# A two-layer encoder in fp32 halves on one core: modulation in 1 MB units, norm chains without other work in them, the MLP in three parts

## The chip, the core and the metric

The kernel runs on one core of a Trainium2 chip. The metric is the device time of one execution in microseconds, read as the median of several runs. The engines are called by their names in the profile: PE (TensorE, matmuls), PEld (its weight loads), DVE (VectorE), ACT (ScalarE), POOL (GpSimd) and SP (SyncE, whose one queue issues every transfer here).

## The reference

One sequence of 256 tokens with 2048 features passes through two layers. Cut to what matters:

```python
c_act = jax.nn.silu(c)
for layer in range(2):
    mod = c_act @ ada_w[layer] + ada_b[layer]            # 2048 x 12288
    sh1, sc1, g1, sh2, sc2, g2 = jnp.split(mod, 6, axis=-1)
    h = rmsnorm(x, norm_mix[layer]) * (1.0 + sc1) + sh1
    proj = h @ w_in[layer]                               # 2048 x 4608
    ...  # 8 heads of differential attention, 8 of windowed attention
    x = x + g1 * (jnp.concatenate([out_a, out_b], -1) @ w_out[layer])
    h2 = rmsnorm(x, norm_mlp[layer]) * (1.0 + sc2) + sh2
    x = x + g2 * (jnp.square(jax.nn.relu(h2 @ w_up[layer])) @ w_down[layer])
return rmsnorm(x, final_norm)                            # D_FF is 8192
```

All of it is float32. The weights and the modulation matrices are read once, 581.66 MB in all.

## The kernel before, in words

**Layout and arithmetic.** The activations lie transposed: features on the 128 partitions, the 256 tokens along a row. The residual stream is eight tiles of two 128-feature chunks each (`X`, in the trace `x`). A matmul in full precision is made of cheaper ones: each operand is cut into a high half, rounded to fp32r, and a low half that is the rest. For weights `split` makes them: ACT casts the high half (L367, `whi`), DVE subtracts it from the raw tile (L368, `wlo`). A weight tile is 0.5 MB, 128 x 1024. `gemm` (L383) loads one tile after another, splits it and gives each to PE; for the kind "s", which all the MLP uses, PE makes two products for each 128 columns: the high half times both halves of the activations (L408, 512 columns) and the low half times the high one (L410, 256 columns). It takes the chunks of the contraction in groups of four. `grouped_gemm` (L710) runs several column blocks over groups of chunks, and `settle` adds up what the groups gave.

**Modulation.** The product of the conditioning vector and the modulation matrix isn't made on PE: DVE multiplies a tile of the matrix by the activated vector, spread over the partitions, and sums each row in one operation (L255, `tensor_tensor_reduce`), which gives 128 values of the modulation. A unit of 128 outputs is 1 MB; `ada_job` (L237) loads it in two halves of 0.5 MB and sums them one after the other, the second starting from the first one's result. There are 384 halves. They are spread through the program by a planner: `feed` (L272) is called after every weight tile and issues the next half when enough credit has gathered; `pace` sets the credit per tile so that a goal (the table `GOALS`, in halves issued) is reached at the end of a stage; `cap` holds the planner back ahead of a group; `need` (L280) issues at once what a step must have.

**A layer.** `mixer` (L766) norms `x`, modulates it, projects it (in groups of 2, 4, 4 and 6 chunks in layer 0, all 16 in layer 1), makes the attention and projects back; `residual` (L752) adds the result to `x` with four DVE operations for each pair of chunks (L761). `mlp` (L838) does the hidden 8192 features in two parts of 4096 (`PARTS`): up projection, squared relu (`fin_up`: one DVE operation at L854, then a cast on ACT and a subtraction on DVE in `hilo`), down projection, `residual`.

**The norm chain.** In the last pass of a stage `residual` also squares each finished tile (`square_sum`, L526: ACT squares, DVE adds the first six up, L534, and PE makes the means, L541). `norm_x` (L545) then makes the reciprocal root: two ACT operations and four of DVE (L552 to L555). `modulated` (L573) applies it chunk by chunk: for the first tile in two halves, DVE multiplies (L585), ACT makes the high half (L589), ACT or DVE the exact value (L593, L591), DVE the low half (L595). PE waits for this ahead of every mixer and MLP.

**Buffers and order.** Weight tiles and modulation halves share the six buffers of `rawp`; the split halves have eight in `wp`, the activations 24 in `bp`. The order on each engine is made by a scheduler from the program's order and priorities (`tc.high_priority` for the norm chain); SP issues the loads in its order and stops where a load's buffer isn't free, with all later loads behind it. A sum, a split and a residual step that stand on DVE in one order run in that order.

## Time and profile before

| | |
|---|---|
| runs | 2314.43 us median of 3 (2310.29 to 2318.74) |
| profiled execution | 2310.85 us, of which the span of the trace is 2309.1 |
| mean granted clock of PE | 0.98 of 2.4 GHz |
| busy | PE 2191.3 us (95%), PEld 1894.8, DVE 1808.1 (78%), ACT 1061.2 (46%) |
| transfers | 585.96 MB, 254 GB/s over the span |
| chain that ended last | PE 83%, DVE 4%, ACT 2%, DMA 1% |

PE is busy nearly all the time; the rest of the span has to be looked for stage by stage. The rows below come from five views. The windows give for each stretch its length, then each engine's busy us with its number of instructions in brackets, then the granted clock of PE as a share of full speed, the share of the DMA engines' time that packets took, and GB/s. The groups give line, engine, operation, the output and input tiles and their shapes, the count, then busy us and the mean of one in ns, then the idle time ahead of them and what ended it. The timelines give the start in the span, the length, and in brackets the idle time of that engine just before and its releaser. The DMA issues give the tiles, the queue, how many, the size and the median time from issue to landing. In the first layer the mixer lies in about 0 to 450 us and the MLP behind it up to 1195; the second layer's mixer runs to 1567, its MLP to 2295.

### The profile page before, as it was taken

To read this page: it belongs to the slowest core of one execution; us is meant where nothing else is said; L and a number is where in the kernel's file an instruction comes from. 1 tells how busy PE (TensorE), PEld (TensorE's weight loads), DVE (VectorE), ACT (ScalarE), POOL (GpSimd) and SP (SyncE) were. 2 spreads that over 40 slices of the span, in tenths; PEclk is the share of its full clock that TensorE was granted. 3 is DMA by queue.
4 is the path that set the end of the run, shared out by engine and by line. 5 is a ranking of instruction groups with operands and counts; after the bars stand their busy time and mean duration, and the time that the engine had idled before them with its cause. 6 is when DMAs were issued, how large, how long until landed. Compare 5 with 4: busy or idle time off the path is not lost.

```text
span 2309.1 us, 33300 instructions
## 1 busy us (share of the span) xinstructions
PE 2191.3 (95%) x12540; PEld 1894.8 (82%) x12540; DVE 1808.1 (78%) x2698; ACT 1061.2 (46%) x1521; POOL 0.2 (0%) x4
## 2 busy tenths in 40 slices
...
GB/s 324 327 311 275 217 255 201 293 329 301 204 274 316 316 317 328 314 338 348 312 302 192 246 182 157 211 290 236 297 282 233 185 195 186 192 191 187 195 184 110
DMA packets 162450, 585.96 MB, mean 254 GB/s; under 512 B 18289, under 2 KB 18801, under 8 KB 162289
## 3 DMA queue, kind: packets, MB, share of 16 engines
...
HBM read 581.66 MB, written 2.10 MB: 253 GB/s over the span
## 4 chain that ended last, share of the span: by engine, by line
PE 83%; DVE 4%; ACT 2%; issue 1%; DMA 1%; ACTq 0%; DVEq 0%
PE acc L408 48%; PE acc L410 25%; PE acc L381 2%; PE acc L379 2%; PE acc L380 2%; PE misc L616 1%; DVE wlo L368 1%; PE lg L631 1%; DVE araw L255 1%; DVE x L761 1%; PE misc L608 1%; PE lg L680 1%; DMA raw<-in_w_up_dram 0%; ACT whi L367 0%; PE misc L562 0%
## 5 line engine op out<-in xcount | busy, mean ns | idle before, releaser
L408 PE MATMUL acc<-b,whi 128*128 128x512 f32 x4992 | 1742.5, 395 | 38.8 <-DVE b L595 29.4
L410 PE MATMUL acc<-b,wlo 128*128 128x256 f32 x4992 | 1377.1, 281 | 5.0 <-DVE wlo L368 4.8
L408 PEld LDWEIGHTS acc<-b,whi 128*128 128x128 f32 x4992 | 933.4, 188 | 249.2 <-issue 38.0
L367 ACT CAST whi<-raw 128x1024 fp32r<-128x1024 f32 x711 | 726.7, 1052 | 871.8 <-PE acc L408 540.0
L368 DVE TENSOR_TENSOR wlo<-raw,whi 128x1024 fp32r<-128x1024 f32 x711 | 851.9, 1222 | 321.5 <-ACT whi L367 319.4
L410 PEld LDWEIGHTS acc<-b,wlo 128*128 128x128 f32 x4992 | 943.5, 189 | 25.1 <-DVE wlo L368 11.9
L255 DVE CUSTOM_DVE_ANT_0 araw<-araw,c_act,vecs 128x1024 f32<-128x1024 f32 x192 | 249.1, 1303 | 43.5 <-DMA araw<-in_ada_dram 43.3
L255 DVE CUSTOM_DVE_ANT_0 araw<-araw,c_act,mod 128x1024 f32<-128x1024 f32 x192 | 249.1, 1303 | 35.5 <-DMA araw<-in_ada_dram 35.1
L761 DVE SCALAR_TENSOR_TENSOR x<-acc,mod,x 128x256 f32<-128x256 f32 x256 | 112.9, 480 | 24.1 <-PE acc L410 22.1
L379 PE MATMUL acc<-b,whi 128*128 128x256 f32 x320 | 92.1, 291 | 2.9 <-ACT whi L367 2.9
L380 PE MATMUL acc<-b,whi 128*128 128x256 f32 x320 | 91.8, 290 | 0.0
L381 PE MATMUL acc<-b,wlo 128*128 128x256 f32 x320 | 89.4, 293 | 2.5 <-DVE wlo L368 2.4
L487 ACT COPY tmp<-acc 128x256 f32<-128x256 f32 x120 | 44.5, 372 | 64.6 <-PE acc L410 64.3
L488 DVE TENSOR_TENSOR tmp<-tmp,acc 128x256 f32<-128x256 f32 x152 | 62.0, 418 | 14.0 <-ACT tmp L487 13.8
L498 ACT CAST b<-tmp 128x512 fp32r<-128x512 f32 x72 | 44.8, 623 | 49.8 <-DVE tmp L854 48.9
L379 PEld LDWEIGHTS acc<-b,whi 128*128 128x128 f32 x320 | 62.6, 196 | 4.9 <-ACT whi L367 3.3
L381 PEld LDWEIGHTS acc<-b,wlo 128*128 128x128 f32 x320 | 61.1, 197 | 5.3 <-DVE wlo L368 4.0
L380 PEld LDWEIGHTS acc<-b,whi 128*128 128x128 f32 x320 | 62.7, 196 | 1.1 <-issue 1.0
L380 PE MATMUL acc<-wlo,b 128*128 128x512 f32 (+1 forms) x152 | 56.6, 372 | 3.1 <-DVE wlo L368 3.0
L530 ACT ACTIVATE tmp<-x 128x512 f32<-128x512 f32 x35 | 21.7, 631 | 75.7 <-DVE x L761 68.3
L381 PE MATMUL acc<-whi,b 128*128 128x512 f32 (+1 forms) x152 | 55.9, 367 | 0.0
L499 DVE TENSOR_TENSOR b<-tmp,b 128x512 fp32r<-128x512 f32 x72 | 49.3, 688 | 7.1 <-ACT b L498 6.2
(156 smaller groups left out, 1258.6 us busy)
## 6 DMA issues: line engine op xcount, KB each, us to landing
araw<-in_ada_dram SPq DMA_DIRECT2D x384, 512.0 KB, 5.2
raw<-in_w_up_dram SPq DMA_DIRECT2D x256, 512.0 KB, 4.5
raw<-in_w_down_dram SPq DMA_DIRECT2D x256, 512.0 KB, 4.6
raw<-in_w_in_dram SPq DMA_DIRECT2D x144, 512.0 KB, 4.7
raw<-in_w_out_dram SPq DMA_DIRECT2D x64, 512.0 KB, 4.7
...
```

What stands on the lines that cost most here:

```text
L255: nc.vector.tensor_tensor_reduce(raw, raw, c_act[:, hf * RAW : (hf + 1) * RAW], scale=scale, scalar=m[:, ch : ch + 1] if hf else vecs[:, b ...
L367: nc.scalar.copy(hi, raw)
L368: nc.vector.tensor_tensor(lo, raw, hi.bitcast(F32), op=ALU.subtract)
L379: nc.tensor.matmul(o, lhsT=lhi, rhs=rhi, start=first, stop=False, skip_group_check=True)
L380: nc.tensor.matmul(o, lhsT=lhi, rhs=rlo, start=False, stop=False, skip_group_check=True)
L381: nc.tensor.matmul(o, lhsT=llo, rhs=rhi, start=False, stop=last, skip_group_check=True)
L408: nc.tensor.matmul(bank, lhsT=hi[:, fs], rhs=act[:, :, aj, :], start=first, stop=False, skip_group_check=True)
L410: nc.tensor.matmul(bank[:, 1, :], lhsT=lo[:, fs], rhs=act[:, 0, aj, :], start=False, stop=last, skip_group_check=True)
L488: nc.vector.tensor_add(tj, tj, b[:, 1, :])
L498: nc.scalar.copy(hl[:, 0], src)
L499: nc.vector.tensor_tensor(hl[:, 1], src, hl[:, 0].bitcast(F32), op=ALU.subtract)
L761: nc.vector.scalar_tensor_tensor(x[:, j, :], sums, g[j], x[:, j, :], op0=ALU.mult, op1=ALU.add)
```

## The change

**Units of modulation.** A unit is one load of 1 MB (128 x 2048) and one sum (now L258). The units have two buffers of their own in `rawp`; weight tiles have four, the split halves nine, the activations 21. All goals count units, so they are halved, and some are moved: the layer 0 mixer's stay where they were until its last one, which rises from 120 halves to 64 units.

**Norm chain.** `norm_x` has three DVE operations. At the start of the kernel nothing is added on DVE: all eight squares go to PE. The last square of a stage is made in two halves. The first modulated tile is made wholly on DVE. The first block of a projection behind a norm is issued `behind` the last operations of the chain, activations are fetched as they are needed with two tiles of look-ahead (`OnDemand`, `LOOK`), the last block ahead of a norm issues no modulation unit (its rate is 0), and the first two weight tiles of the next projection are loaded and split ahead of the norm (`load_ahead`).

**MLP.** The hidden features are done in parts of 3072, 3072 and 2048. In layer 0 ACT makes the relu and both squares (`hilo_square`), and DVE only the low half.

The rest (`WHOLE_MIXED` by pair) has an empty table and changes nothing that runs. The diff, cut:

```diff
-PARTS = (4, 4)
+PARTS = (3, 3, 2)
...
-RAWB, WB = 6, 8
-GOALS = [((72, 96, 120), (160, 204, 248, 304)), ((316, 326, 352), (384, 384, 384, 384))]
+BPB, RAWB, ADAB, WB = 21, 4, 2, 9
+AHEAD = 2
+FIRST_DVE = True
+BEHIND = True
+LOOK = 2
 SQ_ADDED = 6
+RELU_ACT = {0}
+GOALS = [((36, 48, 64), (84, 102, 110, 126, 138, 152)), ((158, 163, 176), (192,) * 6)]
...
-        for hf in range(2):
-            for sec, ch in rows:
...
-                raw = rawp.tile([P, RAW], F32, tag="raw", name=nm("araw"))
-                nc.sync.dma_start(raw, ada[l, sec, ch, hf])
...
+            raw = rawp.tile([P, D], F32, tag="araw", name=nm("araw"), bufs=ADAB)
+            nc.sync.dma_start(raw, ada[l, sec, ch])
...
+            nc.vector.tensor_tensor_reduce(
+                raw, raw, c_act, scale=scale, scalar=vecs[:, b0 : b0 + 1], op0=ALU.mult, op1=ALU.add, accum_out=m)
...
+    def load_ahead(w, c0):
+        for row in range(0, 2 * AHEAD, 2):
+            ahead[(id(w), c0, row)] = load(w, c0, row)
...
+            acts[min(u + LOOK, n - 1)]
+            key = (id(w), c0, rows[u])
+            hl = ahead.pop(key) if key in ahead else load(w, c0, rows[u], not acts[u][1])
...
+    def hilo_square(r):
+        hl = bslot()
+        nc.scalar.activation(hl[:, 0], r, AF.Square)
+        nc.scalar.activation(r, r, AF.Square)
+        nc.vector.tensor_tensor(hl[:, 1], r, hl[:, 0].bitcast(F32), op=ALU.subtract)
+        return hl
...
-    def square_sum(i):
+    def square_sum(i, added=SQ_ADDED):
...
+        if i == n - 1:
+            for j in range(2):
+                nc.scalar.activation(sq[:, j, :], X[i][:, j, :], AF.Square)
...
-        nc.scalar.activation(y, a, AF.Exp, scale=-0.5)
-        nc.vector.tensor_mul(a, y, y)
-        nc.vector.scalar_tensor_tensor(a, ms, EPS, a, op0=ALU.add, op1=ALU.mult)
-        nc.vector.tensor_scalar(a, a, -0.5, 1.5, op0=ALU.mult, op1=ALU.add)
-        nc.vector.tensor_mul(r, y, a)
+        last_op[1] = nc.scalar.activation(y, a, AF.Exp, scale=-0.5)
+        nc.vector.scalar_tensor_tensor(a, ms, EPS, y, op0=ALU.add, op1=ALU.mult)
+        nc.vector.scalar_tensor_tensor(a, a, -0.5, y, op0=ALU.mult, op1=ALU.mult)
+        last_op[0] = nc.vector.scalar_tensor_tensor(r, a, 1.5, y, op0=ALU.add, op1=ALU.mult)
...
-            if not whole:
+            if not whole and i == 0 and FIRST_DVE:
+                nc.vector.tensor_scalar(hi[:, j, :], t[:, j, :], G, sh, op0=ALU.mult, op1=ALU.add)
+            elif not whole:
...
-            if (l, sec) in V_DVE:
-                nc.vector.tensor_scalar(v[:, j, :], t[:, j, :], G, sh, op0=ALU.mult, op1=ALU.add)
+            if (l, sec) in V_DVE or (i == 0 and FIRST_DVE):
+                last_op[0] = nc.vector.tensor_scalar(v[:, j, :], t[:, j, :], G, sh, op0=ALU.mult, op1=ALU.add)
...
+            if gi == 0 and norm is not None and BEHIND:
+                acts[0]
+                front.enter_context(behind(last_op))
...
                 for i in range(NCH // 2):
-                    square_sum(i)
+                    square_sum(i, 0)
...
-        rate = pace(goals[2], 32)
+        rate = pace(goals[2], 28)
...
+                final = part == 1 and c0 + 512 == D
+                banks = gemm(w_out[l], c0, 512, rows, acts, "s", 0.0 if final else rate)
+                if final:
+                    load_ahead(w_up[l], 0)
...
+                if l in RELU_ACT:
+                    nc.scalar.activation(r, r, AF.Relu)
+                    u.append(hilo_square(r))
+                    continue
...
-            rate = pace(goal, n * 2)
+            rate = pace(goal, n * 2 - (n // 2 if final else 0))
...
+                quiet = final and nb == 3
+                banks = gemm(w_down[l], nb * 512, 512, rows, acts, "s", 0.0 if quiet else rate)
+                if quiet and l + 1 < DEPTH:
+                    load_ahead(w_in[l + 1], KA)
```

How this moves instructions shows at three places. In the rows below `araw` is a tile of the modulation matrix, `mod` its sums, `x` the residual tiles, `misc` the PSUM bank with the mean of the squares, `b` the norm and the modulated chunks, `tmp` what lies between.

The first place is the order on DVE ahead of layer 0's MLP, around the norm's own steps. Before:

```order
L255 ISA araw_4217,mod_3315<-araw_4217,c_act,vecs 128x1024
L255 ISA mod_3315 128x1
L552 TENSOR_TENSOR b_4169<-b_4169 128x256
L255 ISA araw_4220,mod_3325<-araw_4220,c_act,vecs 128x1024
L255 ISA mod_3325 128x1
L553 SCALAR_TENSOR_TENSOR b_4169<-misc_4049,b_4169 128x256
L255 ISA araw_4223,mod_3315<-araw_4223,c_act,mod_3315,vecs 128x1024
L255 ISA mod_3315 128x1
L554 TENSOR_SCALAR b_4169<-b_4169 128x256
L255 ISA araw_4226,mod_3325<-araw_4226,c_act,mod_3325 128x1024
L255 ISA mod_3325 128x1
L555 TENSOR_TENSOR b_4169<-b_4169 128x256
```

Of the change, from the last residual steps (L811) through the norm (L597 to L599) and the first modulated tile (L629 to L641) to the second's first step (L631):

```order
L811 SCALAR_TENSOR_TENSOR x_107<-acc_3904,mod_1338,x_107 128x256 x2
L597 SCALAR_TENSOR_TENSOR b_4022<-misc_3898,b_4022 128x256
L598 SCALAR_TENSOR_TENSOR b_4022<-b_4022 128x256
L599 SCALAR_TENSOR_TENSOR b_4022<-b_4022 128x256
L629 TENSOR_TENSOR tmp_4028<-x_93,b_4022 128x256 x2
L633 TENSOR_SCALAR b_4029<-tmp_4028,mod_2800,mod_3142 128x256
L637 TENSOR_SCALAR tmp_4030<-tmp_4028,mod_2800,mod_3142 128x256
L633 TENSOR_SCALAR b_4029<-tmp_4028,mod_2800,mod_3142 128x256
L641 TENSOR_TENSOR b_4029<-tmp_4030,b_4029 128x256
L637 TENSOR_SCALAR tmp_4030<-tmp_4028,mod_2800,mod_3142 128x256
L641 TENSOR_TENSOR b_4029<-tmp_4030,b_4029 128x256
L631 TENSOR_TENSOR tmp_4043<-x_95,b_4022 128x512
```

The sums of modulation (L255) that stood between the norm's steps, as others did among the residual steps ahead of them, are gone from there; the next sum stands behind the last row shown.

The second place is the order on DVE ahead of layer 1's mixer. Before:

```order
L368 TENSOR_TENSOR wlo_11114<-raw_11111,whi_11113 128x1024
L368 TENSOR_TENSOR wlo_11152<-raw_11149,whi_11151 128x1024
L255 ISA araw_11199,mod_10543<-araw_11199,c_act,vecs 128x1024
L255 ISA mod_10543 128x1
L552 TENSOR_TENSOR b_11020<-b_11020 128x256
L368 TENSOR_TENSOR wlo_11158<-raw_11155,whi_11157 128x1024
L553 SCALAR_TENSOR_TENSOR b_11020<-misc_10603,b_11020 128x256
L554 TENSOR_SCALAR b_11020<-b_11020 128x256
L555 TENSOR_TENSOR b_11020<-b_11020 128x256
L585 TENSOR_TENSOR tmp_11027<-x_93,b_11020 128x256 x2
L591 TENSOR_SCALAR tmp_11029<-tmp_11027,mod_7239,mod_7299 128x256
```

Of the change, first the end of the residual steps, then the end of the first modulated tile and what follows:

```order
L811 SCALAR_TENSOR_TENSOR x_107<-acc_10432,mod_4733,x_107 128x256 x2
L258 ISA araw_12916,mod_10068<-araw_12916,c_act,vecs 128x2048
L258 ISA mod_10068 128x1
L811 SCALAR_TENSOR_TENSOR x_107<-acc_10433,mod_4733,x_107 128x256 x2
L597 SCALAR_TENSOR_TENSOR b_10639<-misc_10427,b_10639 128x256
```
```order
L637 TENSOR_SCALAR tmp_10647<-tmp_10645,mod_6150,mod_6204 128x256
L258 ISA araw_13154,mod_10020<-araw_13154,c_act,vecs 128x2048
L258 ISA mod_10020 128x1
L641 TENSOR_TENSOR b_10646<-tmp_10647,b_10646 128x256
L631 TENSOR_TENSOR tmp_10660<-x_95,b_10639 128x512
L258 ISA araw_10669,mod_10068<-araw_10669,c_act,vecs 128x2048
L258 ISA mod_10068 128x1
L637 TENSOR_SCALAR tmp_10662<-tmp_10660,mod_6150,mod_6204 128x256 x2
```

The splits in and ahead of the chain are gone from it; three sums stand in it, one ahead of the last residual steps, one ahead of the second low half and one ahead of the second tile's modulation.

The third place is the start of the kernel, in SP's order of loads behind those of `x`. Before, where four loads of halves stand ahead of these rows:

```order
L308 DMA b_171<-in_diff_lambda_dram 128x512
L311 DMA sinks<-in_swa_sink_dram 128x16
L248 DMA araw_214<-in_ada_dram 128x1024
L248 DMA araw_217<-in_ada_dram 128x1024
L248 DMA araw_220<-in_ada_dram 128x1024
L248 DMA araw_223<-in_ada_dram 128x1024
L451 DMA raw_236<-in_w_in_dram 128x1024
L248 DMA araw_238<-in_ada_dram 128x1024
L248 DMA araw_241<-in_ada_dram 128x1024
L451 DMA raw_244<-in_w_in_dram 128x1024
L248 DMA araw_262<-in_ada_dram 128x1024
```

Of the change:

```order
L252 DMA araw_152<-in_ada_dram 128x2048
L252 DMA araw_156<-in_ada_dram 128x2048
L302 DMA b_159<-in_positions_dram 128x256
L304 DMA rates<-in_consts_dram 128x4
L306 DMA b_163<-in_consts_dram 128x256
L308 DMA b_165<-in_diff_lambda_dram 128x512
L311 DMA sinks<-in_swa_sink_dram 128x16
L387 DMA raw_229<-in_w_in_dram 128x1024
L252 DMA araw_213<-in_ada_dram 128x2048
L252 DMA araw_216<-in_ada_dram 128x2048
L387 DMA raw_234<-in_w_in_dram 128x1024
```

Eight halves of modulation stood ahead of the first weight tile (`raw`); now two whole units do, and one or two stand between the weight tiles after it. On PE the order there before was, first the products that spread the conditioning vector (L221, four for each of its four quarters), then the means of the squares (L541), then the projection:

```order
L221 MATMUL acc_123<-ident,e 128x128 x4
L221 MATMUL acc_129<-ident,e 128x128 x4
L221 MATMUL acc_135<-ident,e 128x128 x4
L221 MATMUL acc_141<-ident,e 128x128 x4
L541 MATMUL misc_196<-b_179,mean_d 128x256 x2
L541 MATMUL misc_196<-tmp_199,mean_d 128x256 x2
L541 MATMUL misc_196<-tmp_203,mean_d 128x256 x2
L377 MATMUL acc_232<-b_227,raw_236 128x256
```

Of the change (L226 spreads the vector, L586 makes the means), the end of the means and what follows:

```order
L586 MATMUL misc_175<-tmp_194,mean_d 128x256 x2
L586 MATMUL misc_175<-tmp_198,mean_d 128x256 x2
L586 MATMUL misc_175<-tmp_202,mean_d 128x256 x2
L226 MATMUL acc_129<-ident,e 128x128 x2
L226 MATMUL acc_135<-ident,e 128x128 x4
L226 MATMUL acc_141<-ident,e 128x128 x4
L377 MATMUL acc_225<-b_220,raw_229 128x256
```

The last ten of the sixteen products of L226 are issued behind the means; DVE's first sum reads the whole vector.

## Rows read from the trace of the kernel before

**Rows 1.** Part 1 of the page: busy time of each engine.
```profile
PE 2191.3 (95%) x12540; PEld 1894.8 (82%) x12540; DVE 1808.1 (78%) x2698; ACT 1061.2 (46%) x1521; POOL 0.2 (0%) x4
```

**Rows 2.** Windows: length, busy of PE, PEld, DVE, ACT, POOL; clock, DMA share, GB/s.
```profile
0.00:60.00 60.00, 34.17 (x116) 25.16 (x116) 40.54 (x79) 15.92 (x28) 0.20 (x4) 0.83 0.89 326
60.00:183.00 123.00, 101.90 (x628) 90.81 (x629) 113.37 (x176) 53.92 (x72) 0.00 (x0) 0.92 0.88 318
...
355.00:440.00 85.00, 80.90 (x456) 68.57 (x455) 81.79 (x151) 39.45 (x63) 0.00 (x0) 1.00 0.74 254
440.00:553.00 113.00, 93.87 (x492) 76.99 (x492) 108.39 (x167) 50.30 (x78) 0.00 (x0) 0.94 0.92 333
...
641.00:1140.00 499.00, 499.00 (x2876) 439.23 (x2875) 430.71 (x577) 206.52 (x236) 0.00 (x0) 1.00 0.90 323
...
1190.00:1220.00 30.00, 20.10 (x97) 16.63 (x96) 25.44 (x52) 14.61 (x25) 0.00 (x0) 0.83 0.37 135
...
1540.00:1600.00 60.00, 46.13 (x243) 37.99 (x242) 58.45 (x101) 28.58 (x40) 0.00 (x0) 0.91 0.67 232
1600.00:2290.00 690.00, 690.00 (x3981) 603.69 (x3980) 418.14 (x500) 293.98 (x356) 0.00 (x0) 1.00 0.63 208
```

**Rows 3.** Groups of DVE, shapes apart: busy us, mean ns | idle before.
```profile
L368 DVE TENSOR_TENSOR wlo<-raw,whi 128x1024 fp32r<-128x1024 f32 x711 | 851.9, 1222 | 321.5 <-ACT whi L367 319.4
...
L255 DVE CUSTOM_DVE_ANT_0 araw<-araw,c_act,vecs 128x1024 f32<-128x1024 f32 x192 | 249.1, 1303 | 43.5 <-DMA araw<-in_ada_dram 43.3
...
L761 DVE SCALAR_TENSOR_TENSOR x<-acc,mod,x 128x256 f32<-128x256 f32 x256 | 112.9, 480 | 24.1 <-PE acc L410 22.1
...
L854 DVE SCALAR_TENSOR_TENSOR tmp<-tmp 128x512 f32<-128x512 f32 x64 | 43.7, 687 | 0.3
```

**Rows 4.** Timeline of PE at layer 0's MLP norm: start, length, instruction, [idle before].
```profile
450.08 0.28 PE L410 MATMUL acc<-b,wlo 128*128 128x256 f32 x1
...
465.26 0.77 PE L408 MATMUL acc<-b,whi 128*128 128x512 f32 x1 [10.93 <-DVE b L595]
```

**Rows 5.** Timeline of all engines, from the last product to the output.
```profile
2294.77 0.28 PE L410 MATMUL acc<-b,wlo 128*128 128x256 f32 x1
...
2296.13 0.63 ACT L530 ACTIVATE tmp<-x 128x512 f32<-128x512 f32 x1 [2.54 <-DVE x L761]
...
2296.81 1.13 PE L541 MATMUL misc<-tmp,mean_d 128*128 128x256 f32 x4 [1.76 <-ACT tmp L530]
...
2298.94 0.43 DVE L552 TENSOR_TENSOR b<-b 128x256 f32<-128x256 f32 x1 [1.79 <-ACT b L551]
...
2300.64 1.89 DVE L892 TENSOR_TENSOR tmp<-x,b 128x512 f32<-128x512 f32 x3
```

**Rows 6.** Timeline of PE at the two norms of layer 1.
```profile
1194.65 0.28 PE L410 MATMUL acc<-b,wlo 128*128 128x256 f32 x1
...
1206.83 0.76 PE L408 MATMUL acc<-b,whi 128*128 128x512 f32 x1 [7.87 <-DVE b L595]
...
1566.73 0.28 PE L410 MATMUL acc<-b,wlo 128*128 128x256 f32 x1
...
1581.21 0.76 PE L408 MATMUL acc<-b,whi 128*128 128x512 f32 x1 [10.58 <-DVE b L595]
```

**Rows 7.** DMA issues in 20:60 and 1900:2000: KB each, median us to landing.
```profile
araw<-in_ada_dram SPq DMA_DIRECT2D x17, 512.0 KB, 5.5
...
raw<-in_w_up_dram SPq DMA_DIRECT2D x30, 512.0 KB, 3.7
```

**Rows 8.** Timeline, start: first sum, first product, end of the twelfth unit.
```profile
12.12 1.34 DVE L255 CUSTOM_DVE_ANT_0 araw<-araw,c_act,vecs 128x1024 f32<-128x1024 f32 x1 [1.93 <-DMA araw<-in_ada_dram]
...
29.32 1.22 PE L377 MATMUL acc<-b,raw 128*128 128x256 f32 x2 [3.81 <-ACT b L593]
...
59.75 0.09 DVE L255 DVE_READ_ACCUMULATOR2_ANT mod<- 128x1 f32 x1
```

133 lines of the change are left out of this document (71 added, 62 removed).

## The prediction

> **What bounds the kernel now.** I began with the busy line of the page [rows 1]. TensorE (PE) is busy 2191.3 of 2309.1 us, so 118 us is all that can go without removing matmuls, and the change removes none. Next I cut the span into stages [rows 2]. In 641:1140 and 1600:2290 PE has no idle microsecond, so nothing done to VectorE (DVE) there can show. The idle time lies in five places. The start (0:60) has 26 us, the rest of the first mixer (60:183) 21, the norm and first up projection of layer 0's MLP (440:553) 19, the norm ahead of layer 1's mixer (1190:1220) 10, and the norm ahead of layer 1's MLP with the projection before it (1540:1600) 14. In 60:183, 440:553 and 1540:1600 DVE is busy for 113 of 123, 108 of 113 and 58 of 60 us: PE waits there because DVE has too much to do, or does it in the wrong order. The unit costs of that work are in the groups of DVE [rows 3]: 1.22 us for a split (the subtraction that makes the low half of a weight tile), 1.30 for a sum over half a modulation unit, 0.48 for a residual step, 0.69 for the squared relu.
>
> The three waits between layers are seen directly. Ahead of layer 0's MLP the last product of the projection starts at 450.08 and the first of the up projection at 465.26 [rows 4], and by the order on DVE at least one sum of 1.3 us stands before each step of the norm chain. The other two holes run from 1194.65 to 1206.83 and from 1566.73 to 1581.21 [rows 6]. The same chain with nothing in between is seen at the end of the kernel: from the last product's start at 2294.77 to the first use of the norm at 2300.64, 5.9 us [rows 5].
>
> I added up the order of before on DVE with each group's mean less 0.07 us, since one instruction's end overlaps the next one's start. That gives 1809.6 us against 1808.1 [rows 1], so I price the changed order in the same way.
>
> **The change, part by part.**
>
> *1 MB sums.* A row of 512 columns takes 0.687 and one of 1024 takes 1.222 [rows 3], so 512 columns more cost 0.535 and 1024 more cost 1.07. A sum over 2048 is then 1.23 + 1.07 = 2.30 us, against 2 x 1.23 = 2.46: 0.16 saved per MB. Bounds: 2.46 (nothing saved) and 2.14 (the columns alone). Over 192 MB that is 31 us of DVE, of which only what falls into DVE-bound stretches counts.
>
> *Start.* The first sum starts at 12.12, the first product at 29.32, and 12 MB are summed at 59.75 [rows 8]. Now all eight squares go to PE and, by the order on PE, ahead of the last products that make the activated conditioning vector; DVE's first sum waits for that vector. Sixteen mean products at 0.43 us end near 14, so the first sum starts near 16 and the second, with a norm step between, ends near 21. From there two buffers of 1 MB carry the rest, each going round in 2.3 (sum) + 0.4 (issue) + landing. A landing of 1 MB isn't in the trace. Half of it lands in 3.7 us when the queue is calm and 5.5 when it is full [rows 7]; another half at the 330 GB/s of 0:60 [rows 2] adds 1.6. So 5.3 to 7.1; I take 5.3, the calm row's, because fewer bytes are queued than with six buffers. Five rounds of 8 us give 12 MB at 61: +1 us. PE starts near 24 rather than 29, but then waits for weights that stand behind the sums' loads on SP, so I count nothing for it. Bounds: -5 (PE keeps its lead) and +10 (7.1 per landing).
>
> The Trainium skill, "DMA: Bandwidth & Descriptors", section "Anatomy of one DMA", gives about 2.0 us plus the bytes at 436 GB/s, hence 4.4 us for 1 MB as an estimate from that page, and the start would then come out at -3 instead of +1. Its section "Bandwidth" measures 6.15 us for 1 MB on another issue path, which would make it +5; no run here shows either.
>
> *First mixer, 60:183.* 16.5 MB x 0.16 on a bound DVE: -3 us.
>
> *Layer 0's out projection, 355:440.* The goal rises to 64 units of 1 MB at its end, where it was 120 halves. For the same 24 splits DVE has 85.0 us instead of 77.4, and was idle 3.2 of the 85 there [rows 2]. Between 0 and +4.4; I take +2.
>
> *Layer 0's norm and first up projection.* Before: 32 splits at 1.15, 41 half sums at 1.23 and 21.6 us of additions and modulation are 108.8 us, and the trace has 108.4 in 440:553, so this stretch is DVE's. PE's share is 88 us (1600:2290 has 3981 products in 690 us, so 8 splits of 64 product pairs take 22). Now three parts leave only 24 splits to hide the same modulation: 27.6 + 15 x 2.30 + 19.9 = 82.0, then 24.6 for the next 8 splits, which belong to the second group. With 3.5 us in which DVE stands idle inside the freed chain that is 110.1, against 112.5: -2 us, although the hole itself shrinks by over 8. Work pushed out of the chain comes back behind it.
>
> *Layer 1's mixer norm.* The freed chain: 5.9 less 0.3 (the last square, 0.63, is made in halves), 0.55 (half of the mean product, 1.13, comes earlier) and 0.43 (one DVE step fewer) [rows 5], plus 2.1 for six DVE steps of 0.35 up to the first low half: about 6.7 us. But the changed order keeps one 2.3 us sum ahead of the last two residual steps (+1.8), one ahead of the second low half and one ahead of the next modulation. PE can take its first 8 product pairs and then waits for these. PE has 0.83 of its clock in 1190:1220 [rows 2], that is, it runs partly at 1.2 GHz, so those pairs stretch and cover part of it; I keep +2.8 (bounds 0 and +4.6, the two sums whole). 12.2 becomes 11.3: -1 us.
>
> *Layer 1's out projection and MLP norm.* Here the sums have been pulled forward, so the projection has none: of its idle time -1.5. The hole of 14.5 becomes 6.7 + 2.6 (one sum ahead of the second modulation): -5. Together -6.5.
>
> *End.* Shorter chain, half square: -1.
>
> *Hidden.* The third part adds 64 residual steps (0.41 start to start, 26 us of DVE) in 641:1140 and 1600:2290, where DVE has 68 and 272 us to spare; without that cover it would be the 26. Relu and a second square add 1.3 us to each of 32 tiles on ScalarE, busy 207 of 499 us there; squaring also takes 0.6 x 32 from DVE.
>
> **Sum:** +1 - 3 + 2 - 2 - 1 - 6.5 - 1 = -10.5 us. The profiled execution took 2310.85 us (span and 1.75 around it), which gives 2300; it lies 3.6 below the median of 2314.43, and against that the forecast is **2304 us**.
>
> **The rivals.**
>
> *Two buffers are too few (slower).* Place: the loads of the modulation units on SP, up to 183 us. A sum frees its buffer only when DVE gets to it, and weights queue behind the load that waits. With a landing of 9 us a round is 11.7: 12 MB at 79.5 (+20), and the next 21 MB at 5.85 us each just keep up with the 123 us that they take now. With the other terms that is 20 - 11.5 = +8.5, and a little more where a sum that waits holds up the splits behind it: 2324 us. It decides from a landing of about 7.4 us, where 5 x (7.4 - 5.05) eats the 11.5. For it: the full queue's 5.5 us per half; against it: less in flight.
>
> *DVE takes everything back (no change).* The order moves sums, hardly removes any; if layer 0 is bound by DVE throughout and the sums in layer 1's chain cost their full 2.3 each, only the last terms stay, about -3: 2311 us.
>
> *The chains are free and nothing returns (much faster).* Then the holes give 8.5 + 5.5 + 7.8, the early start of PE 5 and the end 1, and with the first mixer's 3 that is 31: 2284 us. Against it: the full DVE in 440:553.
>
> **How the numbers follow.** A measurement of this kernel can tell about 0.3% (7 us) from no change. Forecast 0.48, of which 0.08 lies within 0.3%; much faster 0.20; no change 0.14, of which 0.02 lies beyond it on the faster side; slower 0.18, of which 0.02 lies within it. So faster 0.40 + 0.20 + 0.02 = 0.62, same 0.08 + 0.12 + 0.02 = 0.22, slower 0.16. The range takes in the much faster case and its spread, down to 2280, and the slower one up to 2322, leaving out about 0.16, mostly above. The forecast's own range is 2294 to 2312.
>
> **What would show it.** Right: holes of 7 to 9 us ahead of both MLPs and a less improved one ahead of layer 1's mixer, with sums between its steps; PE idle in 355:550 hardly less; sums at about 2.3 us; first product near 24 us. Wrong: sums that wait long for their loads before 60 us, a landing above 7 us, or a first up projection in which PE is no longer held by DVE.

## The result, and the profile after

The changed kernel takes 2340.51 us (median of 6 runs, 2330.81 to 2344.08) against 2316.59 (6 runs, 2310.29 to 2324.06): ratio 1.009, 95% interval 1.0063 to 1.0116 (the two medians alone give 1.010). It is slower by some 24 us where 10 fewer were forecast. The profiled execution has a span of 2342.3 us, 33.2 more than before's. The page's busy line and the main groups of DVE, after:

```profile
PE 2224.2 (95%) x12560; PEld 1909.7 (82%) x12560; DVE 1788.6 (76%) x2330; ACT 1092.4 (47%) x1580; POOL 0.2 (0%) x4
```
```profile
L258 DVE CUSTOM_DVE_ANT_0 araw<-araw,c_act,vecs 128x2048 f32<-128x2048 f32 x192 | 454.2, 2367 | 87.2 <-DMA araw<-in_ada_dram 86.4 <-DVE wlo L368 0.2
L811 DVE SCALAR_TENSOR_TENSOR x<-acc,mod,x 128x256 f32<-128x256 f32 x320 | 147.4, 480 | 29.2 <-PE acc L436 26.1
```

A sum of 2048 columns takes 2.37 us, with 0.07 of overlap the 2.30 of the prediction, and DVE is 20 us less busy than before [rows 1, 3]; the third part shows in 320 residual steps for 256. What is odd stands first in the line: nearly the same products (20 more, for the means) with the same mean clock keep PE busy for 2224 us, 33 more than before. PE's idle time is 118 us in both, so the loss doesn't show there. The windows of [rows 2], for the changed kernel (length, busy of PE, PEld, DVE, ACT, POOL with counts, clock, DMA share, GB/s):

```profile
0.00:60.00 60.00, 38.02 (x128) 27.84 (x128) 30.92 (x48) 14.64 (x26) 0.20 (x4) 0.83 0.81 294
60.00:183.00 123.00, 100.55 (x610) 89.00 (x611) 112.35 (x136) 51.33 (x71) 0.00 (x0) 0.93 0.88 329
...
355.00:440.00 85.00, 80.22 (x435) 66.32 (x435) 81.92 (x150) 39.27 (x77) 0.00 (x0) 0.98 0.69 246
440.00:553.00 113.00, 96.48 (x504) 79.43 (x504) 103.06 (x128) 53.54 (x84) 0.00 (x0) 0.95 0.82 303
...
641.00:1140.00 499.00, 493.68 (x2802) 427.86 (x2801) 405.52 (x428) 226.51 (x276) 0.00 (x0) 1.00 0.89 322
...
1190.00:1220.00 30.00, 28.37 (x161) 24.34 (x159) 24.07 (x31) 9.42 (x11) 0.00 (x0) 1.00 0.82 288
...
1540.00:1600.00 60.00, 53.88 (x295) 46.72 (x294) 46.24 (x76) 23.25 (x29) 0.00 (x0) 0.95 0.47 150
1600.00:2290.00 690.00, 686.51 (x3876) 593.73 (x3875) 436.12 (x512) 294.52 (x360) 0.00 (x0) 1.00 0.62 205
```

Read the counts in brackets and not the busy time. In 1600:2290 PE was busy for 690 us before and is for 686.5 now, but issued 3981 products then and 3876 now. In 60:183 and 355:440 it does less than before, with DVE as full as it was.

The holes are what was forecast, or better. PE's timeline at the three norms, as in [rows 4, 6]:

```profile
463.29 0.28 PE L436 MATMUL acc<-b,wlo 128*128 128x256 f32 x1
...
470.39 0.77 PE L434 MATMUL acc<-b,whi 128*128 128x512 f32 x1 [4.58 <-DVE b L641]
...
1222.51 0.28 PE L436 MATMUL acc<-b,wlo 128*128 128x256 f32 x1
...
1230.08 0.76 PE L434 MATMUL acc<-b,whi 128*128 128x512 f32 x1 [4.58 <-DVE b L641]
...
1588.68 0.28 PE L436 MATMUL acc<-b,wlo 128*128 128x256 f32 x1
...
1595.78 0.76 PE L434 MATMUL acc<-b,whi 128*128 128x512 f32 x1 [4.58 <-DVE b L641]
```

From one last product's start to the next first one it is 7.1, 7.6 and 7.1 us, where it was 15.2, 12.2 and 14.5. At the kernel's end the norm is first used 4.9 us after the last product began, where it took 5.9 [rows 5]:

```profile
2328.94 0.28 PE L436 MATMUL acc<-b,wlo 128*128 128x256 f32 x1
...
2333.84 0.69 DVE L951 TENSOR_TENSOR tmp<-x,b 128x512 f32<-128x512 f32 x1
```

**Two paces of the main products.** A pair of them (512 and 256 columns) started every 346.7 ns on average in nearly all of before's long stretches. In the changed kernel's trace there are stretches at 346.7 and others at 353.3, with almost nothing between. The same 500 us of layer 1's MLP, PE without an idle microsecond and the clock at 1.00, before and after:

```profile
1700.00:2200.00 500.00, 500.00 (x2886) 437.26 (x2885) 287.20 (x332) 210.56 (x252) 0.00 (x0) 1.00 0.61 201
```
```profile
1700.00:2200.00 500.00, 500.00 (x2832) 433.85 (x2831) 286.83 (x329) 201.65 (x238) 0.00 (x0) 1.00 0.59 190
```

2886 and 2832 products: 500/1443 = 0.3465 us a pair, and 500/1416 = 0.3531. Over a layer's 2048 MLP pairs the slower pace costs 13.5 us. Most changes of the value stand at a wait of PE, and some, without a wait, where the order of the products breaks. Of r9 (an experiment below) the first two rows give 349 and 342 products in 60 us on either side of 708 us, with no idle time of PE in either. Between them stands the third, in which two long products follow one another and a short one comes later:

```profile
640.00:700.00 60.00, 60.00 (x349) 52.46 (x348) 48.34 (x49) 22.10 (x22) 0.00 (x0) 1.00 0.90 331
715.00:775.00 60.00, 60.00 (x342) 52.09 (x341) 49.24 (x52) 26.10 (x32) 0.00 (x0) 1.00 0.91 326
```
```profile
707.93 0.62 PE L434 MATMUL acc<-b,whi 128*128 128x512 f32 x2
```

So that stages can be compared, I took from each what its pairs took above 346.7 ns, summed over stretches in which they follow one another without a wait (this is "the pace" below, and what is left is "net"). Net, the loss is 14.8 us of the 33; the pace is 18 of it. All stages come from PE's timeline: from the start to the last product of layer 0's mixer, the hole there, layer 0's MLP, the next hole, and so on. Between two programs a stage can differ by 3 us without any edit to it: the first mixer is 2.9 us longer than before's in r2, and 3.0 longer and 3.0 shorter than the changed kernel's in r3 and r7, whose edits all lie behind it.

| net us (pace) | before | changed | r1 again | r9 | r11 | r10 |
|---|---|---|---|---|---|---|
| first mixer | 450.2 | 463.3 | 463.1 | 447.5 | 456.5 | 438.7 |
| hole | 14.9 | 6.8 | 6.8 | 6.8 | 6.8 | 19.2 |
| layer 0's MLP | 729.4 (0.3) | 745.4 (7.0) | 745.0 (4.2) | 729.6 (5.4) | 740.7 (5.5) | 720.6 (5.8) |
| hole | 11.9 | 7.3 | 7.2 | 12.2 | 7.7 | 11.6 |
| layer 1's mixer | 358.1 (2.1) | 357.9 (1.0) | 358.1 (1.0) | 358.3 (0.6) | 358.1 (1.0) | 363.3 (1.1) |
| hole | 14.2 | 6.8 | 6.8 | 6.8 | 6.8 | 10.3 |
| layer 1's MLP | 713.7 (0.2) | 720.7 (12.7) | 720.6 (12.7) | 720.6 (12.7) | 720.6 (12.7) | 715.0 (0.3) |
| behind it | 14.0 | 13.0 | 13.0 | 13.0 | 13.3 | 14.0 |
| net against before | 0 | +14.8 | +14.2 | -11.6 | +4.1 | -13.7 |

### The profile page after: what moved, and what is told of

Read it like the earlier page. It is cut to its first block, busy times and chain, and to the rows that moved or that the text cites. A ratio compares the mean times of both kernels' runs of the same rounds, so it can differ in the third digit from the quotient of the medians.

```text
span 2342.3 us, 32759 instructions
## 1 busy us (share of the span) xinstructions
PE 2224.2 (95%) x12560; PEld 1909.7 (82%) x12560; DVE 1788.6 (76%) x2330; ACT 1092.4 (47%) x1580; POOL 0.2 (0%) x4
## 4 chain that ended last, share of the span: by engine, by line
PE 56%; DVE 3%; DMA 1%; ACT 1%; issue 1%; DVEq 0%
PE acc L434 34%; PE acc L436 17%; DMA araw<-in_ada_dram 1%; PE acc L379 1%; PE acc L380 1%; PE acc L381 1%; DVE araw L258 1%; PE misc L663 1%; DVE wlo L368 1%; PE lg L678 1%; DVE x L811 0%; PE misc L586 0%; PE misc L655 0%; PE lg L727 0%; DVE tmp L637 0%
## 5 line engine op out<-in xcount | busy, mean ns | idle before, releaser
L434 PE MATMUL acc<-b,whi 128*128 128x512 f32 x4992 | 1768.3, 400 | 35.3 <-DVE b L641 13.7
L436 PE MATMUL acc<-b,wlo 128*128 128x256 f32 x4992 | 1396.8, 283 | 7.5 <-DVE wlo L368 7.4
L436 PEld LDWEIGHTS acc<-b,wlo 128*128 128x128 f32 x4992 | 949.4, 190 | 23.2 <-DVE wlo L368 13.5
L258 DVE CUSTOM_DVE_ANT_0 araw<-araw,c_act,vecs 128x2048 f32<-128x2048 f32 x192 | 454.2, 2367 | 87.2 <-DMA araw<-in_ada_dram 86.4
L811 DVE SCALAR_TENSOR_TENSOR x<-acc,mod,x 128x256 f32<-128x256 f32 x320 | 147.4, 480 | 29.2 <-PE acc L436 26.1
L381 PE MATMUL acc<-b,wlo 128*128 128x256 f32 x320 | 89.3, 290 | 6.4 <-DVE wlo L368 6.3
L380 PE MATMUL acc<-b,whi 128*128 128x256 f32 x320 | 91.4, 288 | 0.0
L379 PE MATMUL acc<-whi,b 128*128 128x512 f32 (+1 forms) x152 | 56.5, 379 | 2.8 <-DVE b L512 2.7
L381 PE MATMUL acc<-whi,b 128*128 128x512 f32 (+1 forms) x152 | 56.8, 374 | 0.0
L635 ACT ACTIVATE b<-tmp,mod,mod 128x256 fp32r<-128x256 f32 x56 | 31.6, 596 | 39.2 <-DVE tmp L631 34.7
L377 PE MATMUL acc<-b,raw 128*128 128x256 f32 x96 | 28.6, 463 | 16.5 <-DVE b L637 9.9
```

The lines of the kernel that those rows point to most:

```text
L258: nc.vector.tensor_tensor_reduce(raw, raw, c_act, scale=scale, scalar=vecs[:, b0 : b0 + 1], op0=ALU.mult, op1=ALU.add, accum_out=m)
L379: nc.tensor.matmul(o, lhsT=lhi, rhs=rhi, start=first, stop=False, skip_group_check=True)
L380: nc.tensor.matmul(o, lhsT=lhi, rhs=rlo, start=False, stop=False, skip_group_check=True)
L381: nc.tensor.matmul(o, lhsT=llo, rhs=rhi, start=False, stop=last, skip_group_check=True)
L434: nc.tensor.matmul(bank, lhsT=hi[:, fs], rhs=act[:, :, aj, :], start=first, stop=False, skip_group_check=True)
L436: nc.tensor.matmul(bank[:, 1, :], lhsT=lo[:, fs], rhs=act[:, 0, aj, :], start=False, stop=last, skip_group_check=True)
```

## The experiments

All times of runs, with the kernel before measured in the same session (medians 2313 to 2319):

| run | median us (range, runs) | ratio (95%) |
|---|---|---|
| r1_again | 2338.8 (2328.6 to 2344.6, 7) | 1.0079 (1.0045 to 1.0113) |
| r2_before_three_parts | 2334.8 (2329.9 to 2342.3, 9) | 1.0079 (1.0052 to 1.0106) |
| r3_relu_dve | 2338.7 (2318.7 to 2346.7, 7) | 1.0068 (1.0028 to 1.0108) |
| r4_halves | 2335.6 (2327.8 to 2344.8, 9) | 1.0077 (1.0050 to 1.0103) |
| r5_chain_only | 2347.0 (2342.5 to 2351.7, 6) | 1.0105 (1.0067 to 1.0144) |
| r6_chain_relu_dve | 2327.6 (2323.2 to 2335.8, 10) | 1.0040 (1.0011 to 1.0068) |
| r7_v_on_act, r8_three_ada | 2338.1, 2302.7 (one each) | |
| r9_three_ada_timed | 2314.2 (2301.7 to 2320.7, 12) | 0.9988 (0.9964 to 1.0011) |
| r10_units_without_chain | 2310.8 (2301.9 to 2319.1, 10) | 0.9988 (0.9962 to 1.0014) |
| r11_two_ada_control | 2330.9 (2319.0 to 2334.4, 10) | 1.0050 (1.0026 to 1.0074) |
| r12_high_first | 2315.7 (2313.6 to 2320.9, 12) | 0.9992 (0.9969 to 1.0015) |
| r13_before_again | 2332.5 (one) | |
| r14_eight_halves | 2331.2 (2315.8 to 2338.0, 10) | 1.0039 (1.0005 to 1.0073) |
| r15_turned_no_chain | 2302.9 (2299.7 to 2306.1, 12) | 0.9939 (0.9910 to 0.9968) |
| r16_turned | 2312.1 (2308.5 to 2315.7, 10) | 0.9973 (0.9942 to 1.0005) |

**r1_again.** The file of the change, unedited.

> The changed kernel once more, nothing edited. In its first trace a pair of main products (512 and 256 columns) takes one of two times, 346.7 or 353.3 ns, and keeps it until PE next waits; 21 us of that execution are pairs at the slower pace, 13 of them in layer 1's MLP. Theory chance: the pace is drawn anew at each restart, so the slow stretches (626 to 726, 881 to 1125, 1639 to 2309) will not all recur, and single executions scatter by 13 us. Theory structure: the changed program itself sets the pace, so the same stretches are slow again and the times stay at 2336 to 2344.

The net stages agree with the first trace within 0.5 us. The pace does not: 729 to 857 is slow now and was fast, 935 to 1097 is fast and was slow; layer 1's MLP is slow again. So it is chance at least in layer 0's MLP.

**r2_before_three_parts.** In the kernel before:

```diff
-PARTS = (4, 4)
+PARTS = (3, 3, 2)
-GOALS = [((72, 96, 120), (160, 204, 248, 304)), ((316, 326, 352), (384, 384, 384, 384))]
+GOALS = [((72, 96, 120), (168, 204, 220, 252, 276, 304)), ((316, 326, 352), (384,) * 6)]
```

> The kernel before with the MLP in parts of 3072, 3072 and 2048 and nothing else changed. If the third part is what costs (its 64 residual steps make PE wait for a free bank), some 5 us in each layer, 2326 us. If it is hidden beside PE, as the prediction had it, the time of before, 2313 to 2318, apart from up to 13 us of pace.

Layer 0's MLP is 741.5 net, 12.1 longer than before, layer 1's 714.1, 0.4 longer. This is neither of the two cases: the third part isn't hidden where DVE carries sums of halves as well, and hidden where it has room. (r10 below has three parts too, and its MLP of layer 0 is shorter than before's; but it has units and other goals besides, so it doesn't price the third part.)

**r3_relu_dve.** `RELU_ACT = set()` in the changed kernel.

> The changed kernel with layer 0's relu and square on DVE again (RELU_ACT empty). If ScalarE's three passes make the banks of the up projections late, the stalls at DVE L510 in layer 0's MLP (4.8 us) go and it is 5 us faster than the changed kernel, 2335. If DVE's load is what makes them late, 32 x 0.6 us more on DVE makes it 0 to 10 us slower, 2340 to 2350.

Layer 0's MLP is 740.9 net, 4.5 shorter as in the first case, but the hole behind it is 12.3, 5.0 longer: the move of the relu to ScalarE is worth nothing in sum.

**r4_halves.** In the changed kernel, `ada_job` of before, and:

```diff
-BPB, RAWB, ADAB, WB = 21, 4, 2, 9
+BPB, RAWB, ADAB, WB = 21, 8, 2, 9
-GOALS = [((36, 48, 64), (84, 102, 110, 126, 138, 152)), ((158, 163, 176), (192,) * 6)]
+GOALS = [((72, 96, 128), (168, 204, 220, 252, 276, 304)), ((316, 326, 352), (384,) * 6)]
```

> The changed kernel with the modulation in halves of 0.5 MB again (eight shared buffers, two sums of 1.3 us each MB, all goals doubled). Theory long sums: a sum of 2.3 us that stands ahead of an eviction or a split is what delays the first mixer (13 us) and layer 0's MLP (5 to 9 us); with halves most of it returns, 2318 to 2328, and by the pace 13 less if layer 1's MLP is fast. Rival, the third part or the chain's hoisted work is the cost: 2336 to 2344, and the first mixer still ends 10 us or more later than before.

The first mixer is 448.3 net, 15 shorter: the units in two buffers did cost that. Whether it is the length of a sum or the number of buffers r4 doesn't tell, since it changes both; r9 and r11 below do. Layer 0's MLP is 755.7, 10 longer than with the units. So half of the theory fell: in the MLP the units help.

**r5_chain_only** and **r6_chain_relu_dve.** r4 with before's buffers, parts and goals; r6 also with the relu on DVE:

```diff
-PARTS = (3, 3, 2)
+PARTS = (4, 4)
-BPB, RAWB, ADAB, WB = 21, 8, 2, 9
+BPB, RAWB, ADAB, WB = 24, 6, 2, 8
...
-RELU_ACT = {0}
+RELU_ACT = set()
```

> The changed kernel with two of its parts undone: the modulation in halves of 0.5 MB and the MLP in two parts, with the buffers and goals of before. What is left is the freed norm chain, the load ahead and layer 0's relu on ScalarE. Times of stages are compared less what pairs of main products took above 346.7 ns. Theory: the units cost the first mixer 15 us, the third part costs layer 0's MLP 12, and the freed chains give 8 + 5 + 7 + 1 of which layer 1's MLP takes 7 back; so this one is 10 to 15 us faster than before, span less pace 2291 to 2297. Rival: the freed chain itself is what costs layer 0's MLP (its hidden work comes back): that stage is again 10 us or more longer than before's 729, and the whole is at most 5 us faster.

> As r5_chain_only, with layer 0's relu and square on DVE as before. If ScalarE's part is worth something where DVE is the bound, layer 0's MLP is 5 to 10 us longer than in r5; if not, within 3 us of it.

For r5 the rival held. The three holes are 6.8 us each, and layer 0's MLP is 777.4 net, 48 longer than before. r6 missed both of its cases: with the relu back on DVE that stage is 755.0, 22 shorter than in r5 and still 26 longer than before. In r5 PE stands still once more 7 us behind the first hole, for a cast that ACT makes (L372):

```profile
471.83 0.79 PE L439 MATMUL acc<-b,whi 128*128 128x512 f32 x1 [5.97 <-ACT whi L372]
```

So the freed chain doesn't pay together with halves. That DVE can't make up in the stage behind what it leaves out in the hole is the likely reason, but no run shows it alone.

**r7_v_on_act.** `V_DVE = {(1, 0)}`.

> The changed kernel with the exact value of layer 1's MLP modulation on ScalarE (V_DVE without its second entry): 14 operations of 0.35 us leave DVE in the first up projection behind that norm, and as many of 0.6 come to ScalarE. The changed kernel gains 7.4 us in the hole there and loses 7 in the stage behind it. Theory: DVE is the bound of the first block (modulation of 16 chunks and 8 splits in 22 us of PE), so the stage gets 3 to 5 us shorter, 716 to 718 less pace. Rival: ScalarE would be the bound then, the stage 724 or more.

720.0 against 720.7: neither. The first 45 us behind layer 1's MLP norm, before and after:

```profile
1581.20:1626.20 45.00, 44.99 (x249) 38.99 (x250) 41.39 (x65) 24.26 (x36) 0.00 (x0) 0.96 0.62 215
```
```profile
1595.80:1640.80 45.00, 41.51 (x212) 33.80 (x213) 44.97 (x62) 24.07 (x34) 0.00 (x0) 0.95 0.68 240
```

That is 37 products fewer, 6.4 us at 0.173 each, with DVE busy throughout. In these 45 us DVE made seven half sums before and makes six whole ones now, 9.1 us and 14.1 us of work:

```profile
L255 DVE CUSTOM_DVE_ANT_0 araw<-araw,c_act,vecs 128x1024 f32<-128x1024 f32 x4 | 5.2, 1289 | 3.4 <-DMA araw<-in_ada_dram 3.3
L255 DVE CUSTOM_DVE_ANT_0 araw<-araw,c_act,mod 128x1024 f32<-128x1024 f32 x3 | 3.9, 1285 | 0.2 <-DMA araw<-in_ada_dram 0.2
```
```profile
L258 DVE CUSTOM_DVE_ANT_0 araw<-araw,c_act,vecs 128x2048 f32<-128x2048 f32 x6 | 14.1, 2347 | 0.0
```

Sums of 2.35 us stand between the modulated tiles that PE waits for (DVE's timeline of the changed kernel; L646 makes a low half):

```profile
1596.94 2.35 DVE L258 CUSTOM_DVE_ANT_0 araw<-araw,c_act,vecs 128x2048 f32<-128x2048 f32 x1
...
1600.46 0.69 DVE L646 TENSOR_TENSOR b<-tmp,b 128x512 fp32r<-128x512 f32 x1
...
1607.68 2.35 DVE L258 CUSTOM_DVE_ANT_0 araw<-araw,c_act,vecs 128x2048 f32<-128x2048 f32 x1
```

The stage gives back 7.0 of the 7.4 us that its hole gained: before, DVE made four splits and three half sums in the hole (8.8 us), now none. But DVE's load alone isn't what holds PE there. In r7 DVE is busy for 42.4 of the first 45 us, 2.6 less than in the changed kernel, and waits 2.4 us for a cast of ACT (L520); PE issues 216 products for 212. What holds the rest stays open.

**r8_three_ada** and **r9_three_ada_timed**, one file, and **r11_two_ada_control**:

```diff
-BPB, RAWB, ADAB, WB = 21, 4, 2, 9
+BPB, RAWB, ADAB, WB = 20, 4, 3, 8
```

In r11 `ADAB` stays 2.

> The changed kernel with three buffers for modulation units in place of two, eight for split halves in place of nine and 20 for activations in place of 21. A unit's load lands in 6.2 to 6.8 us, and DVE waits 12.5 us for units in 60 to 355 where it waited 2.8 before. Theory two buffers: the first mixer, 463 us less pace, gets 8 to 13 us shorter. Rival long sums: it is the length of one sum ahead of a split that costs; it gets less than 4 us shorter.

> The kernel of r8_three_ada once more, timed in five rounds: its single execution took 2302.7 us, its span less the pace was 2294. Theory two buffers: the stages come out as in r8 (first mixer 446, layer 0's MLP 731), and with pace drawn by chance (0 to 20 us an execution, the same for both kernels) the median is 8 to 15 us under that of the kernel before. Rival, that one execution was a lucky one in more than the pace: 2310 to 2320, no difference from before.

> The changed kernel with the other two edits of r8_three_ada and not the third unit buffer: 20 activation buffers and eight split halves. Theory two buffers: nothing is gained, the first mixer is 460 to 466 less pace and layer 0's MLP 742 to 750. Rival, the split halves' odd count or the activations did it: the first mixer 450 or less.

The first mixer is 463 with two buffers, 456.5 with two and the other counts, 447.5 (446.3 in r8) with three; layer 0's MLP 745, 740.7 and 729.6. The third buffer is worth 15.7 us net (9.0 in the first mixer, 6.6 in layer 0's MLP and the hole behind it), the other two edits 10.7. By its own numbers r11 lies between its two cases, r8's first mixer is 17 us shorter where 8 to 13 were expected, with the other two edits in it, and in r9 the stages came out as the theory had them, but not the median. Here is the wait itself: the sums of 60 to 355 us and DVE's idle time ahead of them, before, changed, r11 and r9:

```profile
L255 DVE CUSTOM_DVE_ANT_0 araw<-araw,c_act,vecs 128x1024 f32<-128x1024 f32 x38 | 49.1, 1301 | 1.8 <-DMA araw<-in_ada_dram 1.8
L255 DVE CUSTOM_DVE_ANT_0 araw<-araw,c_act,mod 128x1024 f32<-128x1024 f32 x37 | 47.8, 1302 | 1.0 <-DMA araw<-in_ada_dram 1.0
```
```profile
L258 DVE CUSTOM_DVE_ANT_0 araw<-araw,c_act,vecs 128x2048 f32<-128x2048 f32 x43 | 101.7, 2366 | 12.8 <-DMA araw<-in_ada_dram 12.7
```
```profile
L258 DVE CUSTOM_DVE_ANT_0 araw<-araw,c_act,vecs 128x2048 f32<-128x2048 f32 x43 | 101.7, 2366 | 6.8 <-DMA araw<-in_ada_dram 6.6
```
```profile
L258 DVE CUSTOM_DVE_ANT_0 araw<-araw,c_act,vecs 128x2048 f32<-128x2048 f32 x43 | 101.5, 2363 | 2.0 <-DMA araw<-in_ada_dram 2.0
```

DVE waits 2.8 us in 75 halves, 12.8 in 43 units, 6.8 and 2.0. The queue of SP waits too: it holds the next unit's load (L252), and all loads behind it, until a sum has freed a buffer. In the same 60 to 355 us that is (total, times, longest), for the changed kernel and r9:

```profile
SPq L252 <- DVE mod L258: 91.4, 28, 5.9
```
```profile
SPq L252 <- DVE mod L258: 54.4, 16, 7.9
```

In layer 0's MLP the gain is measured, but its way isn't shown: DVE's waits for units from 470 to 1230 us are 51.8 in the changed kernel, 71.7 in r11 and 53.6 in r9. A unit's load took this long in the changed kernel (60 to 183 us; 6.0 in 20 to 60):

```profile
araw<-in_ada_dram SPq DMA_DIRECT2D x22, 1024.0 KB, 6.8
```

In r8 it took 7.4 us and in r9 too, so three buffers don't make a load land sooner. Against before the net is -11.6, and the median is even with it all the same. The traced execution of r9 drew 19 us of pace; that its median run drew about as much is an estimate. r8 and r9 are the strongest evidence on the pace: one file, layer 1's MLP 720.6 net in both, and these 500 us of it (r8, then r9). They ran on two chips, but r9's twelve runs on one chip spread over 19 us as well.

```profile
1700.00:2200.00 500.00, 500.00 (x2887) 440.84 (x2886) 283.68 (x332) 206.46 (x245) 0.00 (x0) 1.00 0.59 190
```
```profile
1700.00:2200.00 500.00, 500.00 (x2832) 433.55 (x2831) 278.57 (x322) 201.20 (x238) 0.00 (x0) 1.00 0.58 186
```

**r14_eight_halves.** The changed kernel with `WB = 8`.

> The changed kernel with eight split halves in place of nine, nothing else. r11_two_ada_control, with 20 activation buffers besides, had a first mixer of 456.5 and a layer 0 MLP of 740.7 less pace, where the changed kernel has 463 and 745. If the ninth half costs (casts run further ahead of what DVE can follow), this one is as r11, 2325 to 2333. If the activations did it, or the difference is the loads' chance, 460 and 743 or more, 2335 to 2342.

First mixer 455.1, layer 0's MLP 736.7, net +0.9 against before: of the two edits of r11 it is the ninth split buffer that costs, 13.9 us by this trace, and not the activations. By the runs it is less certain: a ratio of 1.0039 against 1.0079 and 1.009, with intervals that overlap. DVE's waits for units in 60 to 355 us fall from 12.8 to 4.5 with this edit alone, and r4, with nine split halves and no units, has a first mixer of 448.3. So the ninth buffer doesn't cost by itself, but beside two unit buffers it does (beside three it wasn't run). Why a buffer more makes those waits longer stays open.

**r10_units_without_chain.** The kernel before with the change's `ada_job`, its parts and goals (halved in `pace` and `feed` as there), and

```diff
-    bp = pool("bp", 24)
+    bp = pool("bp", 20)
-RAWB, WB = 6, 8
+RAWB, ADAB, WB = 4, 3, 8
```

> The kernel before with 1 MB units in three buffers, three parts and the goals of the change, the buffer counts of r8_three_ada, and nothing of the norm chain. What r8 has beyond this is the chain. If the freed chains give what their holes show (8 + 7, less the 7 that layer 1's MLP takes back, and 1 at the end), this one is 8 to 16 us slower than r8, 2302 to 2310 less pace. Rival, a hole is not lost time, since DVE works on in it for the block behind: within 4 us of r8.

Net it is 2.1 us shorter than r9, which has the whole chain besides, with the load ahead and layer 0's relu on ACT. The rival held: the holes are 19.2, 11.6 and 10.3, in sum 15.3 longer than r9's, and the stages around them 18.4 shorter. The units with three buffers, and the parts and goals that go with them, have all of the gain here; the freed chains add none.

**r13_before_again.** The kernel before, unedited.

> The kernel before, nothing edited, for a second trace of it. Its first trace has 2.7 us of slow pairs, while its runs lie between 2304.5 and 2332. Theory chance: long stretches of layer 0's or layer 1's MLP are at 353.3 ns in some executions of this kernel too, so that the time less the pace stays at 2308 whatever the execution takes. Rival, the pace is slow only in the changed kernel: under 4 us of slow pairs again.

It has 26.1 us of pace, slow from 574 to 1105 and from 1607 to 2314, and a net span 1.7 under the first trace's. Its 500 us:

```profile
1700.00:2200.00 500.00, 500.00 (x2833) 433.55 (x2832) 289.71 (x339) 207.66 (x252) 0.00 (x0) 1.00 0.62 199
```

So the slow pace comes in the kernel before as well.

**r12_high_first**, on r9's file; **r16_turned** on it too, and **r15_turned_no_chain** on r10's. In r12 the four long products of a bank come first, then the four short ones; in r15 and r16 every second pair is turned:

```diff
-                        nc.tensor.matmul(bank, lhsT=hi[:, fs], rhs=act[:, :, aj, :],
...
+                        for low in ((1, 0) if k % 2 else (0, 1)):
+                            nc.tensor.matmul(bank[:, 1, :] if low else bank, lhsT=(lo if low else hi)[:, fs],
...
```

> The kernel of r9_three_ada_timed with the order of its main products changed: for each bank first the four products of 512 columns, then the four of 256, where they took turns. The same products, loads of weights and columns. If the two paces (346.7 and 353.3 ns a pair) belong to the alternation of long and short products, a group of eight takes one time alone, and executions scatter less than the 19 us of r9. If the pace is a matter of the restart and not of the order, two paces 2 per cent apart appear again, and the median stays within 5 us of r9's 2314.

> r10_units_without_chain with the main products of every second chunk turned round (512, 256, 256, 512 columns in place of 512, 256, 512, 256). In r12_high_first, where four long ones are followed by four short ones, there was one pace, 350.7 ns a pair, between the two of the alternation, and executions scattered by 7 us. If the two paces belong to strict alternation, the turned order has one as well, with a scatter under 10 us; at 350.7 the median is about 2308, no better than r10's 2310.8, and at 346.7 it is 2297 to 2300, 13 us under r10 and 15 under before. If two paces remain, the scatter stays near r10's 17 us and the median within 4 us of it.

> The same turning in the kernel of r9_three_ada_timed (the changed kernel with three unit buffers): one pace gives a scatter under 10 us and a median of 2298 to 2308; two paces give r9's 2314 within 4 us.

r12 and r15 in the same 500 us:

```profile
1700.00:2200.00 500.00, 500.00 (x2851) 436.93 (x2850) 278.96 (x323) 202.92 (x239) 0.00 (x0) 1.00 0.59 188
```
```profile
1700.00:2200.00 500.00, 500.00 (x2872) 436.39 (x2872) 284.08 (x331) 205.45 (x245) 0.00 (x0) 1.00 0.59 189
```

One pace each: 500/1425.5 = 0.3507 us a pair in r12, 500/1436 = 0.3482 in r15, and 0.348 in r16. All three had one pace and the scatter that this was to give. r16 missed its median: 2312.1, where one pace was to give 2298 to 2308. Executions scatter by 7, 6 and 7 us where r9's scattered by 19, r10's by 17 and before's by 32 in r15's session. r15 beats both kernels: 2302.9 us, 0.9939 of before (0.9910 to 0.9968), some 35 under the changed one by the two ratios.

## Why the prediction was wrong

**The step that failed** is the price of the buffers. The round of the two unit buffers was counted for the start alone, as sum, issue and landing, and nothing was put down for it behind the start ("16.5 MB x 0.16 on a bound DVE: -3"), nor for the split halves going from eight to nine. The runs show both: a third unit buffer takes 15.7 us off (r11 to r9), and going back to eight split halves 13.9 (r14); both at once, with one activation buffer fewer, are 26.4 (the changed kernel to r9). The sum's terms against the net stages, where layer 0's are parted at the same products in both kernels (at 360.7 us, the mixer's last and at 552.5 us in the kernel before):

| term | forecast | measured, net us |
|---|---|---|
| start and first mixer up to its out projection | -2 | +7.5 |
| layer 0's out projection | +2 | +5.6 |
| layer 0's norm and first up projection | -2 | -3.1 |
| the rest of layer 0's MLP ("Hidden") | 0 | +11.0 |
| layer 1's mixer norm, and the mixer | -1 | -4.8 |
| layer 1's out projection and MLP norm | -6.5 | -7.4 |
| layer 1's MLP ("Hidden") | 0 | +7.0 |
| end | -1 | -1.0 |
| sum | -10.5 | +14.8 |

The buffers have to do with the rows of layer 0. The +7.0 of layer 1's MLP is the same with three buffers (r9) and is the second thing missed; it stands under "The chains".

**The round.** It was counted as if DVE took the next sum at once. DVE does splits and modulation between sums, so a buffer comes free late, and the load behind it starts late: SP's queue stood 91.4 us for that in 60 to 355 us, and 54.4 with three buffers. The rival "two buffers are too few" had the place and the sign, but its switch, a landing of 7.4 us, was wrong. I took 5.3 us for a landing, "because fewer bytes are queued than with six buffers". It took 6.0 in 20 to 60 us and 6.8 to 183; but in the second trace of the same file (r1) it took 5.1 and 6.9, and the stages came out the same, and r9 lost nothing at 7.3 and 7.4. So the size of a landing isn't what decided. (In 60:183 the kernel before sums 41 halves, so the 16.5 MB should have been 20.5; the -3 hardly moves.)

At the start PE did as forecast: its first product is at 25.6 us, and at 104 us the two kernels stand level. DVE didn't: its first sum starts at 18.5 us where 16 was forecast, the twelfth unit is summed at 66.9 us (63.4 in r1) where 61 was forecast, and DVE waited 13.1 us for units before 60 us, against 10.7 before and 6.0 in r9. Those waits were named as a sign of being wrong.

```profile
25.59 1.19 PE L377 MATMUL acc<-b,raw 128*128 128x256 f32 x2 [8.00 <-DVE b L637]
```
```profile
66.80 0.08 DVE L258 DVE_READ_ACCUMULATOR2_ANT mod<- 128x1 f32 x1
```

The page "DMA: Bandwidth & Descriptors" of the Trainium skill would have made the start the better for it, with an estimate of 4.4 us from its section "Anatomy of one DMA", whose fit is for loads that GpSimd issues. Here the fastest of 192 loads of a unit took 4.6 us and the median of all was 7.2, and the measurement decides. The 6.15 us that the prediction quotes from that page's section "Bandwidth", for GpSimd's loads too, is nearer to the 6.0 of 20 to 60 us.

**The out projection.** The goal that rises to 64 units was to cost 2 us, at most 4.4. This stretch came out 5.6 us longer, 4.4 in r14 and 9.7 in r9; parting at one product is rough, but all of them are above the 2 taken.

**Buffers beyond the round.** r14 prices the ninth split buffer at 13.9 us; it goes through the first mixer and layer 0's MLP (8.2 and 8.7). That two unit buffers also cost in layer 0's MLP is measured (r11 against r9), and how they do isn't shown. With three buffers and eight halves the change is worth -11.6 net, near the -10.5 forecast, but not by its terms: that is a coincidence.

**The chains.** From the last product's start, as forecast, the holes are 7.1, 7.6 and 7.1 us against about 7, 11.3 and 9.3. For layer 0's MLP the step was right, with its reason: hole and first projection together were to give 2 us and gave 3.1. "Work pushed out of the chain comes back behind it" was written there and not applied to layer 1's MLP, where -5 was taken and 7.0 of 7.4 came back. r10 against r9 says it for all of them. The rival "the chains are free and nothing returns" had the holes nearly right (8.1, 4.6 and 7.4 less, against 8.5, 5.5 and 7.8) and failed on the return; "DVE takes everything back" had the return, but no loss.

**Hidden.** The third part was to vanish beside PE. In layer 1 it does (r2, 0.4 us); in layer 0 it cost 12.1 with halves. With units and three buffers it has no price of its own, since no run has these with two parts.

**The pace** was in no term, and the reading that shut it out was the first one: "PE has no idle microsecond, so nothing done to VectorE (DVE) there can show". Having no idle time doesn't fix a rate. By the medians the changed kernel lost 24 us; 15 are net by its trace, and that the other 9 or so are the slow pace, drawn more often than before did in its runs, is an estimate. Of eight traces with the chain and 1 MB units seven have layer 1's MLP slow; of the three with the chain and halves none; of the four without the chain two. The draw differs between executions of one file (r8, r9), and its odds seem to differ between programs; what sets them stays open.
